# Gate and up as one product of 512 columns, three buffers of gathered rows, and the last two expert blocks placed on chip

## The chip, the cores and the metric

The kernel runs on one core of one Trainium2 chip. The metric is the device time of one execution in microseconds (us), measured over whole executions; a profile is taken of a further execution of the same program. The core has five engines that run their own instruction lists: TensorE (PE; the loading of its weights is listed as PEld), VectorE (DVE), ScalarE (ACT), GpSimd (POOL) and SyncE (SP, which here only issues transfers). Sixteen DMA engines move data between memory and the core's on-chip buffer.

## The reference, cut to what matters

One layer: a token mixer (retention and gated DeltaNet) and, behind it, a mixture of experts. 512 tokens of width 1024 go through the router; each token chooses 8 of 64 experts of inner width 256, and a shared expert is added. The change concerns the experts and what follows them:

```python
def expert_block(args):
    xe, e = args
    return (jax.nn.silu(xe @ w_gate_l[e]) * (xe @ w_up_l[e])) @ w_down_l[e]

yb = lax.map(expert_block, (xb, block_e)).reshape(n_slots, d)
routed = jax.ops.segment_sum(yb * slot_w[:, None], slot_tok, num_segments=t + 1)[:t]
shared = (jax.nn.silu(xt @ w_sh_gate_l) * (xt @ w_sh_up_l)) @ w_sh_down_l
return (routed + shared).reshape(b, l, d)
```

The sum is then normalised by its root mean square, scaled by a vector, and added to the residual stream x.

## The kernel before

The part in question starts at about 700 us. It walks over NE = 64 experts, one block of 128 gathered tokens each, and a 65th block that takes what one overfull expert has left (loop L1419, NE + 2 steps, since each step finishes the block of the step before). A dynamic loop (L1458) would serve further overfull blocks; on this data it runs zero times.

Per expert, SP loads gate, up and down weights of 1 MB each (L1193) into rings of three experts; the 65th comes by an indirect transfer of GpSimd (L1191). Products of float32 are made of three products of a rounded high part and a low part (mm3, L111 to L113). So each weight matrix is converted: ScalarE casts the high part (L1171, `wh`), VectorE subtracts it for the low part (L1173, `wl`), into a ring of seven buffers. GpSimd gathers the token rows with an indirect transfer (L1228, `xg`, six buffers; column 1024 + e of a row holds the token's weight for expert e). TensorE turns them (L1236), and ScalarE and VectorE write the high and low parts (L1238, L1239, `xT`). The projections (L1241) run 24 products of 256 columns for gate and then 24 for up. ScalarE and VectorE make the gated activation `sg` (L1248, L1249), TensorE turns it (L1256), ScalarE copies it (L1258, `aT`), and the down product follows (L1267, eight records of 512 columns in the trace). VectorE and ScalarE scale its halves by the token weight (L1271, L1269), and GpSimd adds the block to a sum in memory with an indirect, accumulating transfer (L1272), alternately to two sums, `accd[0]` and `accd[1]`; blocks 61 to 64 all go to `accd[1]`.

Within step e, in the order of the program: half of the projection of block e, a conversion, the turn of the activation of block e-1, the other half, the activation, a conversion, half of the turn of rows e+2, the down product of e-1 with its scatter, the other half of the turn, and the gather for e+4. A scheduler orders the instructions of an engine from this; each engine then runs its list strictly in order.

At the end `accd[0]` has been read at step 62 (L1453); after the branch around the dynamic loop, `accd[1]` is loaded (L1476), both are added (L1478), squared and summed (L1481), the inverse root is a power on GpSimd (L127), the result is scaled (L1484) and either added to the output by an accumulating transfer (L1486, two tiles of 128 tokens) or added on chip and stored (L1488, L1489, the other two).

## Time and profile before

| | |
|---|---|
| device time, median of 3 runs | 1408.96 us (1408.09 to 1412.23) |
| profiled execution, its own time | 1415.91 us |
| span in the profile | 1414.1 us |
| busy share of the span | PE 94%, PEld 76%, DVE 64%, ACT 46%, POOL 29% |
| moved by DMA | 340.5 MB, 241 GB/s over the span |
| mean granted TensorE clock | 0.971 of full speed |

The span is the time from the first to the last instruction of the profiled execution. Busy shares are means over stages of different kinds; what a change is worth is read in its own stage. "A <- B" in a list of waits says that A stood still until B was done. A chain is followed back from the last instruction, at each step to what released it; "DMA" in it is a transfer from its issue to its landing.

### The profile page before, as it was taken

Reading aid. Unit: us, or ns where it says so; the run is one execution under the profiler, and the core shown is the slowest. Engines: PE = TensorE matmul, PEld = TensorE weight load, DVE = VectorE, ACT = ScalarE, POOL = GpSimd, SP = SyncE. Lnnn points to the kernel's source line nnn. Section 1 sums busy time; section 2 is a strip of 40 time slices with the busy share of each in tenths; the row PEclk is TensorE's granted clock in tenths of the full one; section 3 lists DMA queues with packets and bytes.
Section 4 is the critical chain, followed back from the end, with each engine's and each line's share of the span. In section 5 each row is a group of like instructions: output and inputs, shape, how many; then the busy total and the mean of one; then the engine's idle time right before and its main releaser. Section 6 shows DMA issues by size and latency. Waiting matters only on the chain.

```text
span 1414.1 us, 20716 instructions
## 1 busy us (share of the span) xinstructions
PE 1324.8 (94%) x7848; PEld 1074.7 (76%) x7848; DVE 906.7 (64%) x1270; ACT 653.4 (46%) x926; POOL 409.6 (29%) x330
## 2 busy tenths in 40 slices
PE   6999988899999999999999999999999999999990
PEld 1678866798787777778888787878788888878770
DVE  5645796457676555547668666666666666666543
ACT  5533432553333222334355555555656565555531
POOL 0315544865321000003222222222222222224312
PEclk9899998999999999999999999999999999999995
DMA  7554411102316577575699999999999999999954
GB/s 275 181 141 117 121 56 35 52 16 74 88 49 179 178 214 223 152 259 195 249 386 349 352 370 345 373 351 364 362 366 361 368 364 361 367 364 338 326 183 127
DMA packets 137817, 340.51 MB, mean 241 GB/s; under 512 B 28218, under 2 KB 83038, under 8 KB 112756
## 3 DMA queue, kind: packets, MB, share of 16 engines
q1 hardware_dynamic: 110952, 289.46, 57.2%
q0 software_dynamic: 19584, 38.99, 10.9%
q10 hardware_dynamic: 7180, 10.72, 2.2%
q8 instruction: 63, 1.03, 0.3%
q14 instruction: 38, 0.31, 0.1%
HBM read 326.59 MB, written 48.31 MB: 265 GB/s over the span
## 4 chain that ended last, share of the span: by engine, by line
PE 43%; DMA 7%; issue 1%; ACT 1%; POOL 1%; DVE 0%; DVEq 0%; SPq 0%; ACTq 0%; POOLq 0%
PE cs L1267 13%; PE acc L111 7%; PE acc L113 7%; PE acc L112 7%; DMA w<-in_w_up_dram 4%; PE ci L1236 3%; DMA w<-in_w_gate_dram 2%; PE ci L1066 2%; PE acc L1078 1%; PE acc L1256 1%; DMA w<-acc 1%; POOL fr L127 0%; DMA acc<-y,slots 0%; DMA acc<-y,sl_i 0%; ACT wh L1171 0%
## 5 line engine op out<-in xcount | busy, mean ns | idle before, releaser
L111 PE MATMUL acc<-wh,xT 128*128 128x256 f32 x1040 | 302.2, 291 | 0.0
L113 PE MATMUL acc<-wh,xT 128*128 128x256 f32 x1040 | 291.0, 280 | 0.0
L112 PE MATMUL acc<-wl,xT 128*128 128x256 f32 x1040 | 290.6, 279 | 0.0
L1173 DVE TENSOR_TENSOR wl<-w,wh 128x2048 fp32r<-128x2048 f32 x88 | 201.5, 2291 | 76.2 <-PE acc L112 75.2
L1267 PE MATMUL cs<-wd,aT 128*128 128x512 f32 x520 | 234.6, 594 | 4.5 <-DMA wd<-in_w_down_dram 3.6
L1272 POOL DMA_INDIRECT acc<-y,slots x64 | 101.9, 1593 | 466.5 <-ACT y L1269 427.8
L1171 ACT CAST wh<-w 128x2048 fp32r<-128x2048 f32 x88 | 167.5, 1904 | 99.5 <-PE acc L113 70.2
L111 PEld LDWEIGHTS acc<-wh,xT 128*128 128x128 f32 x1040 | 196.6, 189 | 0.2 <-issue 0.2
L112 PEld LDWEIGHTS acc<-wl,xT 128*128 128x128 f32 x1040 | 196.1, 189 | 0.2 <-issue 0.2
L113 PEld LDWEIGHTS acc<-wh,xT 128*128 128x128 f32 x1040 | 195.5, 188 | 0.0
L1267 PEld LDWEIGHTS cs<-wd,aT 128*128 128x128 f32 x520 | 93.8, 190 | 99.0 <-issue 95.1
L1239 DVE TENSOR_TENSOR xT<-ci,xT 128x512 fp32r<-128x512 f32 x130 | 89.2, 687 | 96.5 <-ACT xT L1238 96.1
L100 ACT CAST wu<-raw 128x1024 fp32r<-128x1024 f32 (+1 forms) x73 | 75.1, 1036 | 104.6 <-DMA raw<-in_w_in_dram 68.0
L111 PE MATMUL acc<-hTx,wu 128*128 128x512 f32 (+1 forms) x296 | 119.6, 404 | 1.5 <-ACT wu L100 1.5
L113 PE MATMUL acc<-hTx,wu 128*128 128x512 f32 (+1 forms) x296 | 117.7, 398 | 1.5 <-DVE wu L107 1.5
L1173 DVE TENSOR_TENSOR wl<-wgu,wh 128x2048 fp32r<-128x2048 f32 x42 | 96.2, 2291 | 34.6 <-PE acc L112 34.4
L112 PE MATMUL acc<-hLx,wu 128*128 128x512 f32 (+1 forms) x296 | 117.1, 396 | 0.0
L107 DVE TENSOR_TENSOR wu<-raw,wu 128x1024 fp32r<-128x1024 f32 (+1 forms) x61 | 78.7, 1299 | 55.4 <-ACT wu L100 55.4
L1171 ACT CAST wh<-wgu 128x2048 fp32r<-128x2048 f32 x42 | 79.8, 1901 | 53.5 <-PE acc L113 35.5
L1236 PEld LDWEIGHTS ci<-ident,xg 128*128 128x128 f32 x520 | 72.5, 191 | 30.6 <-issue 30.2
L1228 POOL DMA_INDIRECT xg<-h2d,slots x64 | 75.5, 1180 | 35.6 <-issue 18.0
L1236 PE MATMUL ci<-ident,xg 128*128 128x128 f32 x520 | 78.7, 275 | 0.1
(493 smaller groups left out, 2374.3 us busy)
## 6 DMA issues: line engine op xcount, KB each, us to landing
wd<-in_w_down_dram SPq DMA_DIRECT2D x64, 1024.0 KB
w<-in_w_gate_dram SPq DMA_DIRECT2D x43, 1024.0 KB
w<-in_w_up_dram SPq DMA_DIRECT2D x43, 1024.0 KB
raw<-in_w_in_dram SPq DMA_DIRECT2D x56, 512.0 KB
wgu<-in_w_gate_dram SPq DMA_DIRECT2D x21, 1024.0 KB
wgu<-in_w_up_dram SPq DMA_DIRECT2D x21, 1024.0 KB
mraw<-in_w_mod_dram SPq DMA_DIRECT2D x32, 512.0 KB
wm<-in_w_mod_dram SPq DMA_DIRECT2D x16, 512.0 KB
```

Source lines behind the costliest of these rows:

```text
L100: nc.scalar.copy(dst, src)
L107: (self.nc.gpsimd if eng == "pool" else self.nc.vector).tensor_tensor(dst, src, hi.bitcast(F32), op=OP.subtract)
L111: mm(out, ah, bh, start=start, stop=False)
L112: mm(out, ah, bl, start=False, stop=False)
L113: mm(out, al, bh, start=False, stop=stop)
L1171: nc.scalar.copy(h[:, i:i + max(n, 1024)], w[:, i:i + max(n, 1024)])
L1173: eng(l[:, i:i + n], w[:, i:i + n], h[:, i:i + n].bitcast(F32), op=OP.subtract)
L1228: nc.gpsimd.indirect_dma_start(xg[:, :], None, self.h2d[:, :], bass.IndirectOffsetOnAxis(ap=ix, axis=0), bounds_check=511, oob_is_err=False)
L1236: nc.tensor.transpose(ps[:, k * 128:k * 128 + 128], xv[:, :, c * 4 + k], self.ident)
L1239: tt(l, ps, h.bitcast(F32), op=OP.subtract)
L1267: nc.tensor.matmul(ps, aT[:, m], wd[:, s], start=k == 0, stop=k == 1)
L1272: nc.gpsimd.indirect_dma_start(self.accd[acc][:, :], bass.IndirectOffsetOnAxis(ap=sx, axis=0), y[:, :], None, bounds_check=511, oob_is_err ...
```

## The change

Gate and up of an expert are converted into one pair of tiles (`GH`, `GL`, two experts deep), so that one product takes 256 columns of gate and 256 of up: 24 products of 512 columns in two halves of 12 (L111 to L113, called by `proj`). The cast is cut into two pieces of 1024 columns (L1188). The gathered rows have three buffers; the weight column is copied out of them (L1390, `wcol`). Blocks up to 62 are scattered as before, the last three of them to `accd[0]`. Blocks 63 and 64 are not scattered: their scaled results are kept as high and low parts (`down_parts`, L1293, L1294), one-hot matrices are made from their token lists (`places`, L1301), and TensorE adds them into place (`finish`, L1315, 32 products of 512 columns). `finish` then adds both sums (L1338), takes squares (L1342) and power (L1346), scales (L1349, one tile on GpSimd, L1345), adds x (L1352) and stores (L1353). All of x is loaded at step 62 (L1553), `accd[1]` at 63 (L1557), `accd[0]` at 64 (L1561). The dynamic loop now stands behind this and would repeat it.

```diff
...
 q = self.pool("mq", bufs=2, side="right", reuse=True)
 cst = lambda n: cons[n]
 xtile = lambda: q.tile([128, 2, 8, 128], F32R, name="xT", bufs=2)
-T8 = lambda name: self.wt8([128, 2048], F32R, name, "b")
-def conv(w, eng, n):
-    h, l = T8("wh"), T8("wl")
-    for i in range(0, 2048, max(n, 1024)):
-        nc.scalar.copy(h[:, i:i + max(n, 1024)], w[:, i:i + max(n, 1024)])
-    for i in range(0, 2048, n):
-        eng(l[:, i:i + n], w[:, i:i + n], h[:, i:i + n].bitcast(F32), op=OP.subtract)
-    return h, l
+self.w8s.close()
+self.w8as.close()
+wp = self.pool("wM", reuse=True)
+GU = [wp.tile([128, 2048], F32, name=f"wgu{i}") for i in range(4)]
+GH = [wp.tile([128, 2, 2048], F32R, name=f"gh{i}") for i in range(2)]
+GL = [wp.tile([128, 2, 2048], F32R, name="gl0"), self.hxpool.tile([128, 2, 2048], F32R, name="gl1", tag="b1")]
 hx = self.hxpool.tile([128, 2, 2048], F32, name="wgu", tag="b0")
-GU = [self.wt8([128, 2048], F32, "w", "a") for _ in range(4)] + [hx[:, 0], hx[:, 1]]
-wd2 = q.tile([128, 2, 2048], F32, name="wd", bufs=1)
-DW = [wd2[:, 0], wd2[:, 1], self.keep.tile([128, 2048], F32, name="wd", tag="k0")]
+GU += [hx[:, 0], hx[:, 1]]
+w2 = q.tile([128, 2, 2048], F32, name="wd", bufs=1)
+DW = [w2[:, 0], w2[:, 1], self.keep.tile([128, 2048], F32, name="wd", tag="k0")]
...
 raw = lambda e, n: DW[e % 3] if n == 2 else GU[(2 * e + n) % 6]
+def convert(e, n):
+    if e > NE:
+        return
+    w, h, l = raw(e, n), GH[e % 2][:, n], GL[e % 2][:, n]
+    for i in (0, 1024):
+        nc.scalar.copy(h[:, i:i + 1024], w[:, i:i + 1024])
+    tt(l, w, h.bitcast(F32), op=OP.subtract)
+    load(e + 3, n)
...
-for e, n in ((0, 0), (0, 1), (1, 0), (0, 2), (1, 1), (2, 0), (1, 2), (2, 1), (2, 2)):
+for e, n in ((0, 0), (0, 1), (1, 0), (1, 1), (0, 2), (1, 2), (2, 0), (2, 1), (2, 2)):
     load(e, n)
...
-xg6, xg3 = q.tile([128, 3, 1088], F32, name="xg", bufs=1), self.hxpool.tile([128, 3, 1088], F32, name="xg", tag="b1")
-xgs = [x[:, i] for x in (xg6, xg3) for i in range(3)]
+xg3 = q.tile([128, 3, 1088], F32, name="xg", bufs=1)
+xgs = [xg3[:, i] for i in range(3)]
...
 def gather(ix):
-    xg = xgs[ng[0] % 6]
+    xg = xgs[ng[0] % 3]
     ng[0] += 1
...
-def proj(out, x, w, first=True):
-    for k in range(8):
+def proj(out, x, e, ks=range(8)):
+    o = out.rearrange("p (n f) -> p n f", n=2)
+    for k in ks:
         s = slice(k * 256, k * 256 + 256)
-        self.mm3(out, x[0][:, k], x[1][:, k], w[0][:, s], w[1][:, s], k == 0, k == 7)
+        self.mm3(o, x[0][:, k], x[1][:, k], GH[e % 2][:, :, s], GL[e % 2][:, :, s], k == 0, k == 7)
...
+def down_half(aT, wd, c):
+    ps = self.pc()
+    for k in range(2):
+        s, m = slice(k * 1024 + c * 512, k * 1024 + c * 512 + 512), slice(k * 128, k * 128 + 128)
+        nc.tensor.matmul(ps, aT[:, m], wd[:, s], start=k == 0, stop=k == 1)
+    return ps
 def down(aT, sx, ws, wd, acc):
     y = self.rawp.tile([128, 1024], F32, name="y", tag="raw")
     for c in range(2):
-        ps = self.pc()
-        for k in range(2):
-            s, m = slice(k * 1024 + c * 512, k * 1024 + c * 512 + 512), slice(k * 128, k * 128 + 128)
-            nc.tensor.matmul(ps, aT[:, m], wd[:, s], start=k == 0, stop=k == 1)
+        ps = down_half(aT, wd, c)
         if c:
             nc.scalar.activation(y[:, 512:1024], ps, AF.Copy, scale=ws)
         else:
...
     nc.gpsimd.indirect_dma_start(self.accd[acc][:, :], bass.IndirectOffsetOnAxis(ap=sx, axis=0), y[:, :], None,
                                  bounds_check=511, oob_is_err=False, compute_op=OP.add)
-cv = {}
-def convert(e, n):
-    if e <= NE:
-        cv[e, n] = conv(raw(e, n), tt, 2048)
-        load(e + 3, n)
+def down_parts(aT, ws, wd, y):
+    for c in range(2):
+        ps = down_half(aT, wd, c)
+        h, l = y[:, c * 512:c * 512 + 512], y[:, 1024 + c * 512:1536 + c * 512]
+        nc.scalar.activation(h, ps, AF.Copy, scale=ws)
+        self.parted = nc.vector.scalar_tensor_tensor(l, ps, ws, h.bitcast(F32), op0=OP.mult, op1=OP.subtract)
+    return y
+def places(oh, row):
+    at = q.tile([128, 4], F32, name="at", bufs=2)
+    for t in range(4):
+        ts(at[:, t:t + 1], row, -128.0 * t, None, op0=OP.add)
+        ts(oh[:, t], cst("r0"), at[:, t:t + 1], None, op0=OP.is_equal)
+def finish(m, x1, blocks):
+    mg = [x[:, 0:1024] for x in xgs] + [self.rawp.tile([128, 1024], F32, name="mg", tag="raw")]
...
+    def place(t, j):
+        oh, y = blocks[j]
+        for c in range(2):
+            if j == 0:
+                PS[t, c] = self.pc() if t == 3 else self.pi() if c else self.pa()
+            for i in range(2):
+                nc.tensor.matmul(PS[t, c], oh[:, t], y[:, i * 1024 + c * 512:i * 1024 + c * 512 + 512],
+                                 start=j == 0 and i == 0, stop=j == len(blocks) - 1 and i == 1)
+    for t in (0, 1):
+        place(t, 0)
+    for t in range(4):
+        if t > 1:
+            place(t, 0)
+        for j in range(1, len(blocks)):
+            place(t, j)
...
+    def add(t):
+        for c in range(2):
+            s = slice(c * 512, c * 512 + 512)
+            then(lambda: tt(m[t][:, s], PS[t, c], m[t][:, s], op=OP.add))
+        self.d("moe", m[t], t)
+        junk = q.tile([128, 1024], BF, name="xT", bufs=2)
+        nc.scalar.activation(junk, m[t], AF.Square, scale=D ** -0.5, accum_out=r[:, t:t + 1])
+        nc.scalar.activation(r[:, t:t + 1], r[:, t:t + 1], AF.Identity, bias=self.eps)
+        if t == 1:
+            nc.gpsimd.tensor_tensor(mg[t], m[t], g2p, op=OP.mult)
+        nc.gpsimd.tensor_tensor(r[:, t:t + 1], r[:, t:t + 1], self.mhalf, op=OP.pow)
+    def scaled(t):
+        then(lambda: tt(mg[t], m[t], g2p, op=OP.mult))
+    def out(t, s, eng):
+        then(lambda: nc.vector.scalar_tensor_tensor(mg[t][:, s], mg[t][:, s], r[:, t:t + 1], x1[t][:, s], op0=OP.mult, op1=OP.add))
+        eng.dma_start(self.out[t * 128:t * 128 + 128, s], mg[t][:, s])
+    whole = slice(0, 1024)
+    add(0)
+    scaled(0)
+    add(1)
+    out(0, whole, nc.sync)
+    add(2)
+    scaled(2)
+    add(3)
+    out(1, whole, nc.scalar)
+    scaled(3)
+    out(2, whole, nc.sync)
+    out(3, slice(0, 512), nc.scalar)
+    out(3, slice(512, 1024), nc.sync)
...
     XG[e] = gather(SL[e])
     if e < NE:
-        W[e] = XG[e][:, 1024 + e:1025 + e]
+        W[e] = None
 def make(e, part):
     if e > NE:
         return
     if part == 0:
         XT[e] = xtile()
+        if W[e] is None:
+            W[e] = q.tile([128, 1], F32, name="wcol", bufs=4)
+            nc.scalar.copy(W[e], XG[e][:, 1024 + e:1025 + e])
     turn(XT[e], part, XG[e])
...
+    self.xrow = sl[0]
...
 x = lambda e: [XT[e][:, h] for h in range(2)]
+halves = lambda e: [raw(e, n)[:, i * 1024:i * 1024 + 1024] for n in range(2) for i in range(2)]
+Y = []
 for e in range(NE + 2):
+    if e == NE:
+        OH = GL[(NE - 1) % 2][:, 0, 0:1024].rearrange("p (b t n) -> p b t n", b=2, t=4)
...
+        places(OH[0], row)
+        places(OH[1], self.xrow)
...
     if e <= NE:
         pgu = self.pa()
-        proj(pgu[:, 0:256], x(e), cv[e, 0])
+        proj(pgu, x(e), e, range(4))
         convert(e + 1, 1)
     if e > 0:
         aT = turn_act(SG[e - 1])
     if e <= NE:
-        proj(pgu[:, 256:512], x(e), cv[e, 1])
+        proj(pgu, x(e), e, range(4, 8))
         SG[e] = act(pgu[:, 0:256], pgu[:, 256:512])
         convert(e + 2, 0)
     make(e + 2, 0)
-    if e > 0:
-        down(aT, SL[e - 1], W[e - 1], raw(e - 1, 2), 1 if e - 1 > NE - 4 else (e - 1) % 2)
+    if e > NE - 1:
+        Y.append(down_parts(aT, W[e - 1], raw(e - 1, 2), GH[(NE - 1) % 2][:, len(Y)]))
+    elif e > 0:
+        down(aT, SL[e - 1], W[e - 1], raw(e - 1, 2), (e - 1) % 2 if e < NE - 2 else 0)
         load(e + 2, 2)
     make(e + 2, 1)
     prepare(e + 4)
     if e == NE - 2:
-        halves = lambda w: [w[:, i * 1024:i * 1024 + 1024] for i in range(2)]
-        m0 = halves(raw(e, 0)) + halves(raw(e, 1))
-        x1 = halves(raw(e + 1, 0)) + halves(raw(e + 1, 1))
+        x1 = halves(NE - 2)
         for t in range(4):
-            nc.sync.dma_start(m0[t], self.accd[0][t * 128:t * 128 + 128])
+            nc.sync.dma_start(x1[t], self.out[t * 128:t * 128 + 128])
+    if e == NE - 1:
+        m1 = halves(NE)
+        for t in range(4):
+            nc.sync.dma_start(m1[t], self.accd[1][t * 128:t * 128 + 128])
+    if e == NE:
+        m = halves(NE - 1)
+        for t in range(4):
+            nc.sync.dma_start(m[t], self.accd[0][t * 128:t * 128 + 128])
+        with tc.issue_after(self.parted.ins):
+            for t in range(2):
+                tt(m[t], m[t], m1[t], op=OP.add)
         for t in range(2, 4):
-            nc.sync.dma_start(x1[t], self.out[t * 128:t * 128 + 128])
+            nc.gpsimd.tensor_tensor(m[t], m[t], m1[t], op=OP.add)
+finish(m, x1, list(zip(OH, Y)))
...
+    places(OH[0], self.xrow)
     xT, xg = xtile(), gather(ix)
     for c in range(2):
         turn(xT, c, xg)
     for n in range(3):
         load(NE, n, wi)
-    w = [conv(raw(NE, n), tt, 1024) for n in range(2)]
+        if n < 2:
+            convert(NE, n)
     pgu = self.pa()
-    for n in range(2):
-        proj(pgu[:, n * 256:n * 256 + 256], [xT[:, h] for h in range(2)], w[n])
-    down(turn_act(act(pgu[:, 0:256], pgu[:, 256:512])), ix, ws, raw(NE, 2), 1)
-m = halves(raw(NE, 0)) + halves(raw(NE, 1))
-r = q.tile([128, 4], F32, name="fr")
-for t in range(4):
-    (nc.scalar if t % 2 else nc.sync).dma_start(m[t], self.accd[1][t * 128:t * 128 + 128])
-for t in range(4):
-    tt(m[t], m[t], m0[t], op=OP.add)
-    self.d("moe", m[t], t)
-    junk = q.tile([128, 1024], BF, name="xT", bufs=2)
-    nc.scalar.activation(junk, m[t], AF.Square, accum_out=r[:, t:t + 1])
-    self.rsqrt(r[:, t:t + 1], r[:, t:t + 1], 1.0 / D, EPS)
-for t in range(4):
-    nc.vector.scalar_tensor_tensor(m[t], m[t], r[:, t:t + 1], g2p, op0=OP.mult, op1=OP.mult)
-    if t < 2:
-        nc.gpsimd.dma_start(self.out[t * 128:t * 128 + 128], m[t], accum_op=OP.add)
-    else:
-        tt(m[t], m[t], x1[t], op=OP.add)
-        (nc.scalar if t % 2 else nc.sync).dma_start(self.out[t * 128:t * 128 + 128], m[t])
+    proj(pgu, [xT[:, h] for h in range(2)], NE)
+    aT = turn_act(act(pgu[:, 0:256], pgu[:, 256:512]))
+    y = down_parts(aT, ws, raw(NE, 2), GH[(NE - 1) % 2][:, 0])
+    finish(m, x1, [(OH[0], y)])
...
```

ScalarE, one step in the middle of the loop; `wh` and `gh` are the high parts of weights. Before:

```order
L1171 CAST wh<-wgu 128x2048
L1258 COPY aT<-acc 128x256
L1248 ACTIVATE sg<-acc 128x256
L1171 CAST wh<-wgu 128x2048
L1238 CAST xT<-ci 128x512
L1269 ACTIVATE y<-cs,xg 128x512
L1238 CAST xT<-ci 128x512
```

After:

```order
L1390 COPY wcol<-xg 128x1
L1188 CAST gh_5609<-wgu_5606 128x1024
L1267 COPY aT<-acc 128x256
L1188 CAST gh_5609<-wgu_5607 128x1024
L1257 ACTIVATE sg<-acc 128x256
L1188 CAST gh_5609<-wgu_5606 128x1024
L1245 CAST xT<-ci 128x512
L1188 CAST gh_5609<-wgu_5607 128x1024
L1282 ACTIVATE y<-cs,wcol 128x512
L1245 CAST xT<-ci 128x512
```

The casts are four instead of two, the weight column stands ahead of the first, and that ahead of `aT`. Three casts now stand behind `aT`.

VectorE at the end, from the last down product on. Before:

```order
L1271 TENSOR_SCALAR y<-cs,sl_w 128x512
L1459 REGISTER_ALU
L1459 COMPARE_AND_BRANCH
L1459 UNCONDITIONAL_BRANCH
L1478 TENSOR_TENSOR w<-w,wgu 128x1024 x3
L126 TENSOR_SCALAR fr<-fr 128x1
L1478 TENSOR_TENSOR w<-w,wgu 128x1024
L126 TENSOR_SCALAR fr<-fr 128x1 x2
L1484 SCALAR_TENSOR_TENSOR w<-w,fr,g2p 128x1024
L126 TENSOR_SCALAR fr<-fr 128x1
L1484 SCALAR_TENSOR_TENSOR w<-w,fr,g2p 128x1024 x3
L1488 TENSOR_TENSOR w<-w 128x1024 x2
```

After, where `m` lies in the `wgu` tiles and `mg` partly in `xg`:

```order
L1294 SCALAR_TENSOR_TENSOR gh_5609<-cs,wcol,gh_5609 128x512 x2
L1564 TENSOR_TENSOR wgu_5604<-wgu_5604,wgu_5606 128x1024 x2
L1294 SCALAR_TENSOR_TENSOR gh_5609<-cs,sl_w,gh_5609 128x512 x2
L1338 TENSOR_TENSOR wgu_5604<-acc,wgu_5604 128x512
L1338 TENSOR_TENSOR wgu_5604<-ci,wgu_5604 128x512
L1349 TENSOR_TENSOR xg<-wgu_5604,g2p 128x1024
L1338 TENSOR_TENSOR wgu_5604<-acc,wgu_5604 128x512
L1338 TENSOR_TENSOR wgu_5604<-ci,wgu_5604 128x512
L1352 SCALAR_TENSOR_TENSOR xg<-xg,fr,wgu 128x1024
L1338 TENSOR_TENSOR wgu_5605<-acc,wgu_5605 128x512
L1338 TENSOR_TENSOR wgu_5605<-ci,wgu_5605 128x512
L1349 TENSOR_TENSOR xg<-wgu_5605,g2p 128x1024
```

The branch (L1459) stood ahead of the sums; now sums, scaling and final pass alternate by tile, and the branch follows behind the rows shown.

GpSimd at the end, from the scatter of the dynamic loop on. Before:

```order
L1272 DMA acc_4919<-y,sl_i 512x1024
L1459 REGISTER_ALU
L1459 COMPARE_AND_BRANCH
L1459 UNCONDITIONAL_BRANCH
L127 TENSOR_TENSOR fr<-fr,mhalf 128x1 x3
L1486 DMA out_dram<-w 128x1024
L127 TENSOR_TENSOR fr<-fr,mhalf 128x1
L1486 DMA out_dram<-w 128x1024
```

After, from the scatter of block 59 on, where `acc_4918` is `accd[0]`:

```order
L1285 DMA acc_4919<-y,slots 512x1024
L1285 DMA acc_4918<-y,slots 512x1024
L1198 DMA wd<-in_w_down_dram,wi 128x2048
L1285 DMA acc_4918<-y,slots 512x1024 x2
L1566 TENSOR_TENSOR wgu_5605<-wgu_5605,wgu_5607 128x1024 x2
L1346 TENSOR_TENSOR fr<-fr,mhalf 128x1
L1345 TENSOR_TENSOR xg<-wgu_5604,g2p 128x1024
L1346 TENSOR_TENSOR fr<-fr,mhalf 128x1 x3
L1571 TENSOR_LOAD nx
```

Ahead of the rows of before stand, outside the loop, the scatters of blocks 61, 62, 63 and 64. The scatters of 63 and 64 and both accumulating stores are gone; two sums and a scaling over 1024 columns stand ahead of the powers.

## Rows read from the trace of the kernel before

**Rows 1.** Busy us by stretch: PE, PEld, DVE, ACT, POOL; clock, DMA share, GB/s

```profile
800.00:900.00 100.00, 100.00 (x655) 81.81 (x654) 66.66 (x61) 57.99 (x70) 26.32 (x20) 1.00 1.01 363
...
1200.00:1300.00 100.00, 99.43 (x652) 81.54 (x652) 65.34 (x57) 57.30 (x68) 29.04 (x20) 1.00 1.00 362
...
1380.00:1414.10 34.10, 1.46 (x4) 0.38 (x2) 12.82 (x15) 5.27 (x9) 8.07 (x7) 0.55 0.47 130
```

**Rows 2.** The chain that ended last, from 1225 us (start, us, what)

```profile
1237.03 3.44 PE cs L1267 x8
...
1247.23 3.44 PE cs L1267 x8
...
1259.27 25.89 DMA w<-in_w_gate_dram
...
1319.03 29.25 DMA w<-in_w_up_dram
...
1377.71 4.65 DMA acc<-y,slots
...
1389.12 8.80 DMA w<-acc
```

**Rows 3.** The waits from 800 to 1250 us (in total, times, longest)

```profile
DVE wl L1173 <- PE acc L112: 91.7, 89, 1.2
```

**Rows 4.** The waits from 1250 to 1360 us

```profile
ACT wh L1171 <- DMA w<-in_w_up_dram: 19.1, 4, 5.7
```

**Rows 5.** Timeline of TensorE in an expert step (start, us, form)

```profile
989.83 0.28 PE L111 MATMUL acc<-wh,xT 128*128 128x256 f32 x1
...
991.47 0.28 PE L113 MATMUL acc<-wh,xT 128*128 128x256 f32 x1
```

**Rows 6.** Timeline of TensorE in an earlier stage with 512 columns

```profile
469.82 0.39 PE L112 MATMUL acc<-hLx,wu 128*128 128x512 f32 x1
...
473.96 0.39 PE L112 MATMUL ci<-yl,wu 128*128 128x512 f32 x1
```

**Rows 7.** Timeline of ScalarE ahead of the down product of 1247.23

```profile
1245.57 0.36 ACT L1258 COPY aT<-acc 128x256 f32<-128x256 f32 x1
```

**Rows 8.** Timeline of GpSimd, a gather behind that product

```profile
1253.58 1.04 POOL L1228 DMA_INDIRECT xg<-h2d,slots  x1 [0.31 <-issue]
```

**Rows 9.** Tile of gathered rows: ns min/median/max, first and last start

```profile
L1236 PE MATMUL ci<-ident,xg x520: 272/274/347, 707.1 to 1357.8; 128*128 128x128 f32 x174
L1228 POOL DMA_INDIRECT xg<-h2d,slots x64: 993/1039/2473, 697.8 to 1317.7; - x64
```

**Rows 10.** Groups by line and form: count, busy us, mean ns, idle before

```profile
L100 ACT CAST wu<-raw 128x1024 fp32r<-128x1024 f32 x72 | 74.9, 1047 | 104.6 <-DMA raw<-in_w_in_dram 68.0 <-DMA raw<-in_w_ret_out_dram 13.3 <-PE acc L113 8.7
...
L1116 POOL TENSOR_TENSOR h<-mix,mrow 128x512 f32<-128x512 f32 x4 | 7.1, 1787 | 5.8 <-DVE mix L1112 2.9 <-PE ci L1019 1.5 <-issue 1.5
...
L1101 DVE TENSOR_TENSOR mix<-acc,mrow 128x512 f32<-128x512 f32 x8 | 5.4, 687 | 15.6 <-ACT ojunk L1100 15.6
...
L1484 DVE SCALAR_TENSOR_TENSOR w<-w,fr,g2p 128x1024 f32<-128x1024 f32 x4 | 5.0, 1281 | 0.7 <-POOL fr L127 0.7
L127 POOL TENSOR_TENSOR fr<-fr,mhalf 128x1 f32<-128x1 f32 x4 | 5.0, 1262 | 14.6 <-DVE fr L126 14.6
...
L1478 DVE TENSOR_TENSOR w<-w,wgu 128x1024 f32<-128x1024 f32 x4 | 4.8, 1221 | 15.0 <-DMA w<-acc 15.0
...
L548 POOL TENSOR_TENSOR QE<-QE,rk 128x512 f32<-128x512 f32 x4 | 4.1, 1039 | 0.0
```

**Rows 11.** Timeline of the end, all engines

```profile
1377.76 3.70 PE L1267 MATMUL cs<-wd,aT 128*128 128x512 f32 x8 [0.82 <-ACT aT L1258]
...
1393.08 2.36 DVE L1478 TENSOR_TENSOR w<-w,wgu 128x1024 f32<-128x1024 f32 x2 [12.55 <-DMA w<-acc]
...
1408.58 0.34 ACTq L1489 DMA_DIRECT2D out_dram<-w  x1
```

**Rows 12.** Timeline of GpSimd near the end, a scatter that waits

```profile
1369.86 1.56 POOL L1272 DMA_INDIRECT acc<-y,slots  x1 [9.02 <-DMA acc<-y,slots]
```

16 lines of the change are left out of this document (15 added, 1 removed).

## The prediction

> **What bounds the kernel now.** I read the profile in this order: busy time by stretch, the chain that ended last, the waits, then timelines of one step and of the end. From 800 to 900 us, and nearly so up to 1300, TensorE is busy without a gap while the DMA engines are busy too, at 363 GB/s [rows 1]. In this stage the kernel walks over the experts, one step every 1247.23 − 1237.03 = 10.20 us [rows 2]. The ten waits listed from 800 to 1250 us name no load; the largest behind TensorE is VectorE waiting for a weight buffer that TensorE still reads [rows 3]. So here TensorE sets the step. After 1257 us the chain leaves TensorE: a gate load takes 25.89 us and an up load 29.25 us to land [rows 2], and from 1250 to 1360 ScalarE stands four times for an up load, 19.1 us in all [rows 4]. The last 100 us of the loop go by the loads. The last expert product ends at E = 1377.76 + 3.70 = 1381.46 [rows 11]; the span ends at 1414.1, so 32.6 us run with TensorE practically idle at a granted clock of 0.55 [rows 1]: a chain of scatter, loads, sums, powers, scaling and stores.
>
> **The change part by part.** (a) Products. Start to start, 256 columns take (991.47 − 989.83)/14 = 0.117 us [rows 5] and 512 columns of the same number type (473.96 − 469.82)/18 = 0.230 us [rows 6]. A step now has 48 × 0.117 = 5.62 us of them and will have 24 × 0.230 = 5.52. Two for one is therefore nearly nothing: 0.10 us a step, 65 steps, 6.6 us at most. The rest of a step (turns, down product) is unchanged.
>
> How much of this lands? Up to 1250 us, 53 of the 65 steps, the loads have room, so TensorE should be about 5 us ahead there. Then the loads set the pace, and they come ahead only as far as the DMA engines, already at a share of 1.01 [rows 1], can take it. Against this, both halves of an expert's weights are now converted in the same step, so up must have landed nearly a step earlier than now. I take −2 us for the loop, between 0 and −6.6; a loss of 2 is possible if the late loads bite earlier.
>
> (b) The gathered rows. Three buffers instead of six do not hold back the gather: the rows of expert e+1 have been read when those of e+4 are fetched. But ScalarE now copies the weight column out of the rows before it casts the first half of the gate weights, and behind that stands aT, for which the down product waits. Queued behind a late gather are thus that cast, aT, and through aT TensorE. A gather goes out 1253.58 − 1247.23 = 6.35 us after a down product starts [rows 2, 8]; aT starts 1.66 us before it (1245.57) [rows 2, 7]. The cast before it is half of what it was, so 1.05 us by the cast of 1024 columns [rows 10], and the copy some 0.2. Two steps of 10.10 us after its own down product the rows must be there by 20.2 − 1.66 − 1.25 = 17.3 us; aT itself lasts 0.36, so with no slack left for it another 1.2 us later: 18.5 us. The gather has 18.5 − 6.35 = 12.1 us. No row gives its landing in the loop. Below it is bounded by the first one, issued at 697.8, its rows turned at 707.1: 9.3 us [rows 9]. Above, the turn now needs the rows just before the down product, 20.4 − 0.45 − 6.35 = 13.6 us, and never waited for them [rows 3]. Between 9.3 and 13.6 I take the lower half, since the first one ran beside loads too, and cost it at nothing. The gain covers that; each us beyond 12.1 would cost 0.5 us a step.
>
> (c) The end. What goes: two scatters in sequence (4.65 us of the chain for the first alone) and 8.80 us of loads behind them [rows 2]. What comes: the parts of the last two blocks, 32 products of 512 columns, and a chain on VectorE. Worked from E: the placing of block 63 stands ahead of the last down product, which moves that by some 1.3 us. The parts of block 64 take two passes over 512 columns, 0.69 each [rows 10], and four products 0.9: the first sum could start at E + 3.7. Do the sums in memory arrive by then? The scatter of block 62 went out at 1369.86 after waiting for its forerunner [rows 12], E − 11.6; landing like the next one, 4.65, it is done by E − 7. The first two loads of the sums were there at 1393.08, 4.0 us after the load's row of 1389.12, the last 8.80 after it [rows 2, 11]: E − 3 and E + 1.8. They are in time.
>
> VectorE then runs 8 sums at 0.69, 3 scalings at 1.22, 3 final passes at 1.28 and two of half that size: 14.4 us if nothing holds it [rows 10]. GpSimd may: it adds sums for two tiles and multiplies one, three passes over 1024 columns. It has none of these in the trace, only 512 columns at 1.04 to 1.79 us, so 2.1 to 3.6 each [rows 10]. Added up in queue order with powers of 1.26 us [rows 10], the first power ends at E + 7.7 to 9.0, the second at E + 11.0 to 13.8; VectorE, which needs the first at E + 7.7, ends at E + 18.1 to 19.5. From the last store's issue to the end of the span were 5.5 us [rows 11]; this gives E + 23.6 to 25.0, against 32.6. The branch around the extra loop now lies behind the stores; it may show for up to 1.5 us. I take −7 for the end, between −3 and −9.
>
> The GPSIMD Engine Reference of the Trainium skill (section 3.1) measures a float32 sum over 2048 columns at 4.5 us, from which 2.25 us for 1024 is an estimate. With it the end would be at the lower bound, E + 23.6, and the time 1 to 2 us shorter. No row shows it; the sum keeps both bounds.
>
> **Sum.** The profiled execution took 1415.91 us with a span of 1414.1; the median of the runs is 1408.96, 7 us below. Loop −2 and end −7 give 1415.9 − 9 = 1406.9 for that execution, and on the median 1408.96 − 9 = 1400.
>
> **The rivals.** *The loop gains nothing.* The DMA engines stand at a share of 1.01 and 363 GB/s all along [rows 1]. If they cannot go faster, a shorter step only makes loads late sooner; only the end gains: 1409 − 7 = 1402. Against it: no wait for a load before 1250 [rows 3]. The Trainium skill's DMA: Bandwidth & Descriptors (section Where 436 GB/s comes from) has memory bind at about 358 GB/s per core, which is this case; the row, at 363, lies just above it.
>
> *The whole gain lands.* The late loads are no harder than now, the loop gives 6.6 and the end 9: 1393.5. For it: TensorE without a gap over hundreds of us. Against: the last stage is paced by loads that land in 25 to 29 us.
>
> *The end gives little.* GpSimd's passes at 3.6 us, sums in memory that land 3 to 5 us late because the loads of x and of both sums now crowd the last steps, and the branch: end −2.5, loop −1, so 1405.5.
>
> *Slower: the late gather.* If gathers land after 12.1 us, ScalarE holds aT and TensorE stops once a step. The loop equals the present one at 12.3 us, and the end's gain is eaten at 12.6. At 13.0 us, 0.45 × 62 steps = 28, less the 7 of the end: 1430.
>
> The fifth, that a product of 512 columns costs two of 256, is already nearly so in (a), and moves the time by 6.6 us at most.
>
> **How the numbers follow.** Forecast (1400) 0.38; loop gains nothing (1402) 0.20; whole gain 0.17; the end gives little 0.16; late gather 0.09. A measurement of this kernel tells about 0.3% (4.2 us) from no change: faster is below 1404.7, slower above 1413.2. Faster: 0.36 + 0.17 + 0.17 + 0.03 = 0.73. Same: 0.02 + 0.03 + 0.13 + 0.02 = 0.20. Slower: 0.07. The range runs from 1388 (whole gain, with part of the late stalls gone) to 1412 (little at the end and a few late gathers).
>
> **What would show it.** Starts of down products 10.1 us apart in the middle; waits of ScalarE for loads from about 1240 on, as long as now; no wait of the weight-column copy for a gather above 0.2 us (a row of it by the ten would be the slower rival); TensorE's last product before the placing at about 1380, and 24 to 26 us from there to the end, VectorE waiting for GpSimd's power once or twice. I am wrong if steps are longer than 10.2 us, or if between that product and the end more than 30 us pass.

## The result, and the profile after

| | before | after |
|---|---|---|
| device time, median (4 runs each) | 1409.72 us (1408.09 to 1412.23) | 1419.55 us (1418.82 to 1421.42) |
| ratio after / before | | 1.0077, 95% interval 1.0052 to 1.0102 |
| profiled execution, its span | 1415.91, 1414.1 us | 1421.42, 1419.6 us |
| start of the first down product | 726.0 us | 726.7 us |
| first down product's start to the last one's end ("the loop") | 655.5 us | 661.8 us |
| from there to the end of the span ("the end") | 32.7 us | 31.2 us |

The change made the kernel 0.8% slower, where 0.6% faster was forecast (1400, between 1388 and 1412). In the profiled executions the 5.5 us more are 0.7 ahead of the experts, 6.3 in the loop, and 1.5 less at the end.

The busy time by stretch, as in [rows 1] (PE, PEld, DVE, ACT, POOL; clock, DMA share, GB/s), of after:

```profile
800.00:900.00 100.00, 100.00 (x419) 71.23 (x418) 66.84 (x61) 62.17 (x100) 45.70 (x20) 1.00 1.01 361
1100.00:1200.00 100.00, 97.26 (x402) 68.21 (x401) 61.23 (x55) 57.33 (x93) 40.98 (x20) 1.00 0.98 353
1200.00:1300.00 100.00, 93.92 (x386) 66.11 (x385) 62.72 (x56) 57.93 (x94) 38.97 (x19) 1.00 0.97 345
1300.00:1380.00 80.00, 75.39 (x302) 52.70 (x301) 48.03 (x51) 39.67 (x65) 27.42 (x14) 0.98 0.86 290
1388.50:1419.60 31.10, 8.30 (x28) 5.99 (x26) 19.88 (x20) 6.47 (x13) 12.66 (x7) 0.69 0.32 122
```

From 800 to 900 us TensorE is busy throughout, as before. Between 1200 and 1300 us it now lacks 6.1 us where [rows 1] lacked 0.6. The waits from 800 to 1250 us (in total, times, longest), as in [rows 3], name the reason:

```profile
DVE sg L1258 <- ACT sg L1257: 131.1, 43, 4.9
...
ACT gh L1188 <- DMA wgu<-in_w_up_dram: 50.0, 17, 4.8
```

In before's list no load stood up to 1250 us; now ScalarE stands 17 times for the up weights. The timeline of TensorE shows both regimes in the starts of the down products (start, us, form, idle before and what ended it):

```profile
959.40 3.60 PE L1274 MATMUL cs<-wd,aT 128*128 128x512 f32 x8
969.51 3.60 PE L1274 MATMUL cs<-wd,aT 128*128 128x512 f32 x8
```
```profile
1227.77 3.67 PE L1274 MATMUL cs<-wd,aT 128*128 128x512 f32 x8 [0.33 <-DMA wd<-in_w_down_dram]
1238.97 3.70 PE L1274 MATMUL cs<-wd,aT 128*128 128x512 f32 x8 [0.84 <-ACT aT L1267]
```

At 960 us the step is 10.11 us (10.085 in the mean of two neighbouring steps; [rows 2] gave 10.20). At 1230 us it is 11.20. ScalarE's timeline has the cause inside that long step:

```profile
1226.99 0.35 ACT L1267 COPY aT<-acc 128x256 f32<-128x256 f32 x1
1231.58 1.05 ACT L1188 CAST gh<-wgu 128x1024 fp32r<-128x1024 f32 x1 [4.24 <-DMA wgu<-in_w_up_dram]
1232.54 0.38 ACT L1257 ACTIVATE sg<-acc 128x256 f32<-128x256 f32 x1
```

The cast of the next up weights waits 4.24 us for its load, and the activation stands behind it in ScalarE's list. The first long step starts at 1151 us; the kernel is 4.2 us ahead of before there (down product 42 at 1151.1 against 1155.3), and at down product 63 it is 7.0 us behind (1380.1 against 1373.1).

The end, as in [rows 11], from the last down product on, with the scatter of block 62 ahead of it:

```profile
1379.53 1.55 POOL L1285 DMA_INDIRECT acc<-y,slots  x1 [7.04 <-DMA acc<-y,slots]
...
1384.84 3.62 PE L1274 MATMUL cs<-wd,aT 128*128 128x512 f32 x8
1385.95 2.13 SPq L1561 DMA_DIRECT2D wgu<-acc  x4
...
1389.51 1.22 DVE L1564 TENSOR_TENSOR wgu<-wgu,wgu 128x1024 f32<-128x1024 f32 x1 [4.28 <-DMA wgu<-acc]
1391.76 1.23 DVE L1564 TENSOR_TENSOR wgu<-wgu,wgu 128x1024 f32<-128x1024 f32 x1 [1.02 <-DMA wgu<-acc]
1392.90 1.41 DVE L1294 SCALAR_TENSOR_TENSOR gh<-cs,sl_w,gh 128x512 fp32r<-128x512 f32 x2
...
1393.75 4.74 POOL L1566 TENSOR_TENSOR wgu<-wgu,wgu 128x1024 f32<-128x1024 f32 x2 [12.67 <-issue]
...
1394.53 0.69 DVE L1338 TENSOR_TENSOR wgu<-acc,wgu 128x512 f32<-128x512 f32 x1 [0.23 <-PE acc L1315]
...
1396.53 3.03 DVE L1349 TENSOR_TENSOR xg<-wgu,g2p 128x1024 f32<-128x1024 f32 x1
...
1400.85 3.32 POOL L1345 TENSOR_TENSOR xg<-wgu,g2p 128x1024 f32<-128x1024 f32 x1 [0.85 <-DVE wgu L1338]
...
1411.32 0.33 SPq L1353 DMA_DIRECT2D out_dram<-mg  x1
```

The last down product ends at E = 1388.46. VectorE waits until E + 1.0 for the accumulator (1389.51), holds the parts of block 64 back behind two sums (1392.90), and starts the first sum of `finish` at E + 6.1. The last store goes out at E + 22.9; the span ends 8.3 us later.

### The profile page after: what moved, and what is told of

Read it like the earlier page. It is cut to its first block, busy times and chain, and to the rows that moved or that the text cites. A ratio compares the mean times of both kernels' runs of the same rounds, so it can differ in the third digit from the quotient of the medians.

```text
span 1419.6 us, 17702 instructions
## 1 busy us (share of the span) xinstructions
PE 1326.0 (93%) x6320; PEld 1005.0 (71%) x6320; DVE 908.8 (64%) x1293; ACT 672.8 (47%) x1126; POOL 513.7 (36%) x326
## 5 line engine op out<-in xcount | busy, mean ns | idle before, releaser
L1188 ACT CAST gh<-wgu 128x1024 fp32r<-128x1024 f32 x260 | 271.7, 1048 | 158.2 <-DMA wgu<-in_w_up_dram 87.3
L1189 DVE TENSOR_TENSOR gl<-wgu,gh 128x2048 fp32r<-128x2048 f32 x130 | 297.2, 2287 | 36.6 <-ACT gh L1188 31.1
L1235 POOL DMA_INDIRECT xg<-h2d,slots x64 | 147.2, 2300 | 314.4 <-DVE y L1284 176.7
L111 PE MATMUL acc<-gh,xT 128*128 128x512 f32 x520 | 215.3, 414 | 0.0
L113 PE MATMUL acc<-gh,xT 128*128 128x512 f32 x520 | 204.8, 394 | 0.0
L112 PE MATMUL acc<-gl,xT 128*128 128x512 f32 x520 | 203.8, 392 | 0.0
L1285 POOL DMA_INDIRECT acc<-y,slots x63 | 133.4, 2118 | 95.4 <-ACT wcol L1390 40.0
L1258 DVE TENSOR_TENSOR sg<-sg,acc 128x256 f32<-128x256 f32 x65 | 27.4, 421 | 193.5 <-ACT sg L1257 193.3
L111 PE MATMUL acc<-hTx,wu 128*128 128x512 f32 (+1 forms) x296 | 118.7, 401 | 2.8 <-ACT wu L100 1.5
L113 PE MATMUL acc<-hTx,wu 128*128 128x512 f32 (+1 forms) x296 | 117.0, 395 | 2.0 <-DVE wu L107 2.0
L113 PEld LDWEIGHTS acc<-gh,xT 128*128 128x128 f32 x520 | 97.6, 188 | 22.2
L111 PEld LDWEIGHTS acc<-gh,xT 128*128 128x128 f32 x520 | 98.8, 190 | 16.7 <-issue 0.2
L112 PEld LDWEIGHTS acc<-gl,xT 128*128 128x128 f32 x520 | 98.2, 189 | 16.8 <-issue 0.2
L1245 ACT CAST xT<-ci 128x512 fp32r<-128x512 f32 x130 | 75.8, 586 | 0.0
```

What stands on the lines that cost most here:

```text
L111: mm(out, ah, bh, start=start, stop=False)
L112: mm(out, ah, bl, start=False, stop=False)
L113: mm(out, al, bh, start=False, stop=stop)
L1188: nc.scalar.copy(h[:, i:i + 1024], w[:, i:i + 1024])
L1189: tt(l, w, h.bitcast(F32), op=OP.subtract)
L1235: nc.gpsimd.indirect_dma_start(xg[:, :], None, self.h2d[:, :], bass.IndirectOffsetOnAxis(ap=ix, axis=0), bounds_check=511, oob_is_err=False)
```

## The experiments

Times and lengths in us. A time is a median of 4 to 10 runs, or of one where the table says "1 run"; "before there" is before on the same chip and in the same session (its median, or one run beside e8 to e11 and e15). The lengths come from one profile each: "step" is the mean from down product 5 to 35, of which in e9 alone some are held up; "loop" and "end" are as above.

| kernel | time | before there | step | loop | end |
|---|---|---|---|---|---|
| before | 1409.72 | | 10.21 | 655.5 | 32.7 |
| after | 1419.55 | 1409.72 | 10.10 | 661.8 | 31.2 |
| half_a, half_b (1 run) | 1395.80, 1402.56 | 1407.54 | 10.10, 10.21 | 643.2, 650.5 | 29.4, 32.6 |
| e1_late | 1414.22 | 1407.54 | 10.10 | 662.7 | 29.0 |
| e2_nofor | 1412.22 | 1407.54 | 10.10 | 660.8 | 27.4 |
| e5_aslow (1 run) | 1423.82 | 1410.24 | 10.23 | 666.6 | 31.0 |
| e6_bfast (1 run) | 1406.41 | 1410.24 | 10.09 | 652.4 | 31.1 |
| e7_front | 1405.97 | 1410.24 | 10.28 | 658.1 | 26.9 |
| e8_bgather3 (1 run) | 1417.06 | 1412.04 | 10.24 | 652.2 | 32.4 |
| e9_scatfirst (1 run) | 1448.73 | 1412.04 | 10.77 | 698.0 | 28.8 |
| e10_apart (1 run) | 1419.49 | 1409.03 | 10.30 | 666.6 | 26.8 |
| e11_places (1 run) | 1415.63 | 1409.03 | 10.10 | 662.1 | 30.0 |
| e12_turned | 1400.02 | 1407.14 | 10.10 | 643.2 | 31.1 |
| e13_bturned (1 run) | 1408.07 | 1407.14 | 10.21 | 650.5 | 31.2 |
| e14_best | 1397.18 | 1407.14 | 10.10 | 643.2 | 27.4 |
| e15_by16 (1 run) | 1395.53 | 1407.56 | 10.10 | 643.2 | 27.0 |

The experts begin between 718 and 731 us in profiles of kernels that are the same up to there; so the loop and the end are compared, and not the times of single runs.

**Is it the loads?** Both kernels with half of each down load from expert 3 on; the other half of the down weights stays what it was.

```diff
-nc.sync.dma_start(t, a[NAMES3[n]][0, e].rearrange("(p k) f -> p (k f)", p=128))
+c = 1024 if n == 2 and e > 2 else 2048
+nc.sync.dma_start(t[:, 0:c], a[NAMES3[n]][0, e].rearrange("(p k) f -> p (k f)", p=128)[:, 0:c])
```

> The changed kernel with only the first half of each down weight loaded (experts 3 to 63; the second half of the buffer is stale, so the down products are of wrong data): one sixth of the loads is gone. If late loads are what stretches the steps after 1150 us (theories W and D alike): all steps 10.06 to 10.11 us to the end, last down product ending at about 1370, 18 us below the changed kernel. If something else stretches them (a late gather, TensorE itself): steps of 10.5 to 12 us stay.

> The kernel before with only the first half of each down weight loaded (as in half_a, wrong data in the down products). Late loads as the limit of its last 100 us: all steps 10.2 us, last down product ending at about 1376 instead of 1381.5. Together with half_a it gives the loop's gain where loads have room: 63 steps of 0.12, so 7 to 7.5 us in favour of the changed kernel; if the 512-column product gains nothing by itself, 0.

All steps are then equal, and the loops take 643.2 and 650.5 us. So late loads cost before 5.0 us of its loop and after 18.6; and the joint product with room to run is worth 7.3 us.

**The conversions' place in the queue** (e1_late): the casts of both halves stand behind the activation and the second turn, so that a late load holds neither.

```diff
-                convert(e + 2, 0)
+                with tc.issue_after(self.silu.ins):
+                    convert(e + 2, 0)
...
+            with tc.issue_after(self.turned.ins):
+                convert(e + 2, 1)
```

> The changed kernel with only the order of conversions altered: both casts of gate are queued behind the activation of the step, both casts of up behind the second turn of the step, two steps ahead of their use as before; nothing is left out. Theory W (window): the loop lost 11 us after 1150 us because the casts, cut in halves and tied to the halves of the projection, hold a weight buffer some 10.7 us for up (first cast to end of subtraction) instead of about 4.3, so that a load must land within 22 to 23 us, and a late one stands in ScalarE's queue ahead of the activation. Then the last down product ends at 1380 to 1383 us instead of 1388.5, steps are still 10.09 us until about 1220, and the time is 5 to 8 us below that of the changed kernel (1412 to 1415). Theory D (rate): the DMA engines cannot serve a step of 10.09 us, whatever the order; then the last down product stays within 2 us of 1388.5 and the time within 2 us of 1419.5.

The loop stays at 662.7: the loads themselves are late, whatever stands behind them. The time fell further than theory D allowed, to 1414.22 (before there took 2.2 us less, too), but not in the loop; the end is 2.2 us shorter in its profile.

**The pace** (e5_aslow adds to after a 256-column product a step, overwritten at once; e6_bfast leaves one 256-column product per expert out of before):

```diff
+            if ks[0] == 0:
+                nc.tensor.matmul(o[:, 0], x[0][:, 0], GH[e % 2][:, 0, 0:256], start=True, stop=True)
```

> The changed kernel with one product of 256 columns more in each step (its result is overwritten at once, so nothing is left out): the undisturbed step goes from 10.09 to about 10.2 us, as before. From the first to the end of the last down product the kernel before took 655.5 us, the changed one 661.8. Theory P (pace): what hurts is that a shorter step asks for the loads faster than the slowest DMA engine serves them, and the late loads then cost more than the pace gave; at 10.2 us this stretch falls back to 655 to 657 us. Theory Q (pattern): the changed kernel's order of transfers (three loads within 3.5 us, gather and scatter apart) burdens the slowest engine whatever the pace; the stretch stays at 661 us or more.

> The kernel before with one product of 256 columns left out per expert (the high-by-low product of one eighth of gate, so its result is slightly off): the undisturbed step goes from 10.20 to 10.09 us. Theory P: the stretch from the first to the end of the last down product grows from 655.5 to 659 us or more, long steps beginning well before 1257 us. Theory Q: it stays at 655 us or less, the loads being as early as before.

After at before's step still has its long steps, from about 1140 us on (666.6); before at after's step gains 3 us. Asking for weights faster is not enough to lose time. It does eat up part of what it gains: 63 steps of 0.13 us less should have given before 8 us. Without long steps e6_bfast's loop would be about 650.5 − 8 = 642.4 us and e5_aslow's about 643.2 + 8 = 651.5 (estimates from half_b, half_a and the steps), so long steps cost them some 10 and 15 us.

**Parts of the change** (e8_bgather3 gives before three gather buffers and the copied weight column; e10_apart takes the joint product of after apart again; e11_places swaps two allocations of after):

```diff
-self.mm3(o, x[0][:, k], x[1][:, k], GH[e % 2][:, :, s], GL[e % 2][:, :, s], k == 0, k == 7)
+self.mm3(out, x[0][:, k], x[1][:, k], GH[e % 2][:, n, s], GL[e % 2][:, n, s], k == 0, k == 7)
```

> The kernel before with the gather side of the change alone: three buffers, the weight column copied out by ScalarE; nothing left out. The stretch from the first to the end of the last down product was 655.5 us before and 661.8 changed. Theory G (gather side: three buffers, the copy, GpSimd's queue): it grows to 659 us or more here, with steps over 10.3 us beginning before 1250 us. Theory H (weights' side: pair tiles, split casts, order and closeness of the loads): it stays within 1.5 us of 655.5.

> The changed kernel with the 512-column products taken apart again: the gate product whole, then the up product whole, 256 columns each, in the order of the kernel before, but out of the paired tiles, with three buffers of gathered rows, the weight column's copy and the new end. Full function. Theory S (the joint product itself makes the loads slower: both halves of a pair are read over the whole step): undisturbed steps of 10.21 us, hardly any long steps, first down product to last 652 to 656 us. Theory B (what came with it, the paired tiles' places, the gather's buffers and the column's copy): steps of 10.21 us and long steps from about 1140 us on as in the changed kernel, 661 to 667 us.

> The changed kernel with the order of two allocations changed: the converted pairs stand ahead of the four loaded weight tiles in the pool, so that loads and casts write to other addresses of the scratchpad. Nothing else differs. If the addresses make the loads slower: first down product to last is off from 661.8 by more than 4 us, and where the loads get quicker, 650 to 656 us. If they don't: 660 to 664 us and long steps from about 1140 us on.

652.2, 666.6 and 662.1 us: neither the gather's buffers nor the joint product nor those addresses make the loads later. Before with the gather's side alone came out 3.3 us shorter, below what either of its theories had expected; why was not looked into. Taken apart, the products cost the loop another 4.8 us.

**The late gather** (e9_scatfirst: after with each scatter ahead of the next gather on GpSimd):

```diff
-            prepare(e + 4)
+                with tc.issue_after(self.scat.ins):
+                    prepare(e + 4)
```

> The changed kernel with GpSimd's queue in the order of the kernel before: the scatter of a step ahead of its gather (nothing left out). Theory G: the stretch shrinks from 661.8 to 658 us or less. Theory H: it stays within 1.5 us of 661.8. A third way: the later gather holds the weight column and with it the activation, steps above 10.15 us from the start, and the stretch grows beyond 664.

The wait list from 800 to 1250 us has what the rival of that name described:

```profile
ACT wcol L1390 <- DMA xg<-h2d,slots: 132.0, 35, 7.4
```

The step grows to 10.77 us and the loop by 36 us. In after this wait does not occur; there the gathers land in time (issue to landing, 800 to 1250 us, from the view of the tile `xg`):

```profile
DMA to landing us min/median/max: 7.8/10.3/12.6
```

**Which part of a load is late?** A load of 1 MB reports its landing in 16 parts. The Trainium skill's DMA: Bandwidth & Descriptors (section Why a DMA increments its semaphore by 16 and not by 1) says that these are the 16 DMA engines, which finish independently; the events of this trace agree in that the 16 parts come at times of their own. The parts of expert 43's down load, us after its issue, sorted:

```
before    6.6  6.6  6.6  6.6  6.8  7.1  7.8  8.6  8.9  9.2  9.6  9.7 11.3 12.7 16.1 18.1
after     7.3  7.5  7.6  7.6  7.7  7.8  7.8  7.8  7.9  8.1  9.5 10.3 10.5 16.6 24.8 25.1
e12       7.3  7.3  7.4  7.4  7.5  7.8  7.9  8.2  8.5  9.1  9.2  9.5  9.5 10.1 12.2 12.3
e15       7.2  7.3  7.3  7.3  7.4  7.6  8.4  8.5  8.7  8.8  9.2  9.4  9.8 10.1 10.5 12.5
```

In after, 13 engines are through after 10.5 us; three lag, two of them by 17 us. The mean DMA share, 0.98 from 1100 to 1200 us, hides this. Something is dealt unevenly. It is hardly the loads, which the trace shows in 128 equal pieces of 8192 bytes, eight an engine if they are dealt evenly. It can be the gathered and scattered rows: a list has 128 slots, of which 64 hold a token on average, and each half is filled from its first slot on. So the lists were turned round, expert by expert, with nothing else changed (e12_turned on after, e13_bturned on before):

```diff
-nc.vector.tensor_copy(both[0:64, 0:64], first[0:64])
-nc.vector.tensor_copy(both[64:128, 64:128], first[64:128])
+for r in range(4):
+    for h in range(2):
+        rows, c, o = slice(64 * h, 64 * h + 64), 128 * r + 64 * h, (4 * r + 8 * h) % 16
+        nc.vector.tensor_copy(both[rows, c + o:c + 64], first[rows, 0:64 - o])
...
+    nc.tensor.matmul(ps[:, r:64:4], both[:, 128 * r:128 * r + 128], cst("i2")[:, r:64:4], start=True, stop=True)
```

> The changed kernel with the slots of each expert's list turned round: every half of a list begins 0, 4, 8 or 12 slots further on, by the expert's number modulo 4, the second half 8 further than the first. Full function; the same rows, bytes, transfers and instructions in the loop. In the changed kernel 13 of a load's 16 parts land within 11 us of its issue around expert 43 and the last three after 16 to 25 us, so two or three of the 16 DMA engines fall behind; a list fills each half from slot 0, and if slot k is moved by engine k modulo 16, the first engines carry some 5 row pairs an expert and the last 3. Theory U (uneven rows): with the lists turned no engine falls behind by more than some 7 us at expert 43, its down load lands within 17 us, first down product to last takes 644 to 651 us (661.8 in the changed kernel), and the whole 1403 to 1409 us. Theory T (the transfers as a whole got slower with the change, rows don't matter): landing 22 to 27 us, 660 to 664 us, 1417 to 1421 us.

> The kernel before with the same turning of the lists. Full function. Theory U: its late long steps go, first down product to last 650.5 to 652.5 us (655.5 before; 650.5 is what it took with half of each down load), the whole 1404 to 1408 us beside 1409. Theory T: 654.5 to 656.5 us, no change.

Both loops fall to exactly what half the down load gave, 643.2 and 650.5 us: no long step is left. (The one run of e13_bturned took 1408.07 us beside 1407.14 of before there; its 5.0 us show in the loop alone.) The windows of e12_turned:

```profile
1100.00:1200.00 100.00, 100.00 (x419) 71.23 (x418) 66.86 (x61) 62.20 (x100) 45.72 (x20) 1.00 1.01 369
1200.00:1300.00 100.00, 100.00 (x419) 71.23 (x418) 67.37 (x60) 62.20 (x100) 44.42 (x20) 1.00 1.00 369
```

TensorE has no gap left, and the engines together move 369 GB/s where after moved 353 and 345. The ratio of e12_turned to before is 0.9943 (0.9916 to 0.9969).

**How the rows are dealt.** e15_by16 turns every second list by 16 slots only (`o = 16 * r`, r = 0 or 1):

> The changed kernel with every second expert's list turned by 16 slots in both halves, the others as they are. Full function. It tells two maps of slots to DMA engines apart. Map M (engine = slot modulo 16, as e12_turned was reckoned): a turn by 16 changes no engine's rows, so nothing changes: down load of expert 43 landing after 22 to 27 us, 660 to 664 us from first to last down product. Map S (blocks of four slots: the first half of a list goes to engines 0 to 7, the second to 8 to 15, engine by the slot's number over 4, modulo 8): a turn by 16 moves the surplus four engines on, the heaviest engines carry 4.8 rows an expert instead of 5.7: landing within 15 us at expert 43, and 643 to 648 us.

643.2 us: not map M, by which nothing would have changed, but what map S had foretold. Map S is the one that the Trainium skill's DMA: Bandwidth & Descriptors (section The descriptor swizzle) gives for a plain transfer to 128 partitions; here the gathered and scattered rows follow it too. By this map and the reference's own routing of this data, the heaviest engine carries 5.7 rows an expert and the lightest 2.1. With 24 pieces of loads at the trace's mean of 0.335 us and 0.43 us a row (fitted; gather and scatter packets add up to 0.50 in the means) the four slowest engines would be 15.9, 14.6, 8.5 and 6.1 us behind at expert 43 of after; the list above has 17.6, 17.3, 9.1 and 3.0 beyond 7.5. The heights are partly the fit's doing; the pattern of two engines far behind the others is not. Reckoned the same way, slot modulo 16 leaves its worst engine 6.5 us behind, and eight neighbouring slots to an engine leave four engines 55 to 60 us behind.

**The end.** e2_nofor is after without the loop for further blocks, which on this data never runs. e7_front is before's loop with the new end, where that loop stands ahead of the sums and adds on chip, and the scatters alternate to the last. e14_best joins e12_turned with that end.

```diff
-        cnt = nc.values_load(nx[0:1, 0:1], min_val=0, max_val=62)
-        with tc.For_i(0, cnt) as _:
...
-            finish(m, x1, [(OH[0], y)])
```

> The changed kernel without the dynamic loop over further overfull blocks (it runs zero times on this data, so nothing of the work done is missing). Theory F: behind the stores, the branch waits until they have landed and only then does GpSimd begin its closing drain (3.55 us in the trace of the changed kernel, from 1415.25), so the end is 3.5 to 4.5 us earlier: about 1415.5. Rival: the landing of the last store sets the end and the branch hides behind it; then under 1 us.

> The loop of the kernel before (256-column products, six gather buffers) with the changed end (blocks 63 and 64 placed on chip), the scatters alternating to the last so that block 62 need not wait for 61, and the dynamic loop put ahead of the sums, where it adds into them on chip; nothing is left out. If the end's change is good and the loop's is what cost the time: the stretch of the down products stays near 655 us, from the last down product to the end 26 to 28 us instead of 32.7, the time 5 to 6 us below the kernel before. If placing on chip itself gives nothing: within 2 us of the kernel before.

> The changed kernel's loop with turned lists and the end of e7_front: scatters go to the two accumulators in turn to the last, the loop for further blocks stands ahead of the sums and adds on chip, and the residual rows are loaded after it. Full function. Theory U: 644 to 651 us of loop and an end of about 27 us (26.9 in e7_front), 1397 to 1404 us, faster than all full kernels so far. Theory T: 660 to 664 us of loop, 1411 to 1417 us.

e7_front against before: 0.9974 (0.9956 to 0.9991). e14_best: 0.9925 (0.9896 to 0.9955); its 1397.18 us beat both kernels. From the last store's issue to the end pass 8.3 us in each of nine kernels with the branch behind the stores (after, half_a, e1, e5, e9, e10, e11, e12, e15), and 3.6 in e2, e7 and e14. The events of after show why: the engines leave the branch at 1415.2 us, when the last store has landed (1414.9), and only then does GpSimd begin its closing drain of 3.55 us. In e2_nofor the drain begins at 1403.9, ahead of the last store (1407.2). What comes ahead of the store depends on when the accumulator lands. In e15_by16 it is there early (the view begins behind the first of its four loads):

```profile
1361.92 1.37 SPq L1565 DMA_DIRECT2D wgu<-acc  x3
...
1365.22 2.44 DVE L1568 TENSOR_TENSOR wgu<-wgu,wgu 128x1024 f32<-128x1024 f32 x2 [1.73 <-DMA wgu<-acc]
...
1385.44 0.33 SPq L1357 DMA_DIRECT2D out_dram<-mg  x1
```

Its last down product ends at 1366.72 (1363.09 and 3.62). VectorE's sums start before that, and the last store goes out at E + 18.7. In e14_best the loads of the residual come later, the sums start only 2.7 and 3.6 us behind E, and VectorE and GpSimd sum at the same time; E = 1365.96:

```profile
1368.68 5.69 POOL L1594 TENSOR_TENSOR wgu<-wgu,wgu 128x1024 f32<-128x1024 f32 x2 [14.12 <-DMA wgu<-acc]
...
1369.56 5.89 DVE L1592 TENSOR_TENSOR wgu<-wgu,wgu 128x1024 f32<-128x1024 f32 x2 [2.10 <-issue]
...
1389.67 0.33 SPq L1357 DMA_DIRECT2D out_dram<-mg  x1
```

The store goes out at E + 23.7: 5.0 us are lost ahead of the store, and 4.7 gained behind it. With e15_by16's sums and e14_best's branch the end would be 18.7 + 3.6 = 22.3 us, an estimate that no run tested.

## Why the prediction was wrong

**(a) The product: right.** 0.10 us a step from [rows 5, 6]; the steps shrank from 10.21 to 10.10. With room the loop gains 7.3 us, a little above the 6.6 that the text allowed at most.

**(a) "How much of this lands?": the step that failed.** It said that the loads have room up to 1250 us, that TensorE would then be 5 us ahead, and that the loop nets −2. TensorE was 4.2 us ahead, but the loads bit 100 us earlier, from 1151 us, and the loop lost 6.3. The text reckoned room in time, from a list of waits that named no load [rows 3]. A backlog makes no wait until it is used up: in before the down load's last part already landed 10.1 us after issue at expert 15, 13.8 at 35 and 23.2 at 51. The loads of 25.89 and 29.25 us in the chain [rows 2] were its end, and I took them for a trait of the last stage. The DMA share of 1.01 [rows 1] was read as all engines being full, while a few were overfull. "A loss of 2 is possible if the late loads bite earlier" named the sign and the way, not the size.

**The rival "the loop gains nothing"** had the mechanism: a shorter step only makes loads late sooner. It set the loss at nothing, as if the loads' speed were fixed by the memory at 363 GB/s. It wasn't: after itself moved 369 from 1000 to 1100 us, before its long steps, and with the lists turned the 369 holds up to 1300. The figure beside it, about 358 GB/s from the Trainium skill's DMA: Bandwidth & Descriptors (section Where 436 GB/s comes from), is passed in every window shown whose steps are all undisturbed (361 to 369).

**What stays open.** Long steps cost after 18.6 us and before 5.0. A shorter step uses up the room of the loads sooner, and e5_aslow and e6_bfast tell how much that is: before at after's step loses some 10 us, after at before's step some 15. So the shorter step accounts for 4 to 5 of the 13.6 us between the two, and for no loss by itself, as e6_bfast's loop still gained 3. The other 9 to 10 us, which made the gain a loss, are left to the new weight side, by exclusion: e8_bgather3 has the whole gather side of after, the gather ahead of the scatter included, and its loads are not later. The slowest engine's landings of gate loads, expert 8 to 43, are 10.40 us apart in before, 10.29 to 10.45 in e6 to e8, but 10.48 to 10.60 in after, e1, e2, e5, e10 and e11. So in these single profiles it is slower, by some 0.1 us an expert, in every kernel with the paired tiles, at any pace, with the joint product or without (e5, e6 and e7 ran on one chip); the nearest two of the groups are 0.03 apart. Which part of the new weight side does it was not found. With even lists no load is late enough to make a long step.

**(b) The gather: right.** It cost nothing: its instruction goes out 4.8 us behind a down product (6.35 was reckoned), its rows land 12.6 us later at most, and the weight column never waited for them from 800 to 1250 us. That these rows load some of the DMA engines more than others, and so make the weights late, was not thought of, and that decided.

**(c) The end: −7 forecast, −1.5 measured.** Counted from the end of the last down product, the sum had 2.4 + 14.4 + 5.5 = 22.3 us at the least and the trace has 6.1 + 16.8 + 8.3 = 31.2. (That is one profile; kernels with the same end have 26.8 to 31.2. The 1.3 us by which the placing was to move the last down product came to 0.1: 1384.84 − 1380.12 = 4.72, and in before 1377.76 − 1373.12 = 4.64.) Three terms failed. First, the accumulator "in time": the scatter of block 62 was put at E − 11.6 and went out at E − 8.9 (1379.53, after 7.04 us for its forerunner); its loads followed at 1385.95, 6.4 us later and not 4.65. VectorE therefore started its first sum at E + 6.1, and not at the 2.4 (3.7 from the old E) of the text, with the parts of block 64 queued behind sums in memory. Where the accumulator was early (e15_by16) the last store went out at E + 18.7; the text's 18.1 to 19.5 from the old E is 16.8 to 18.2 from the new. Second, the branch: up to 1.5 us forecast, for which no row stood; with it 8.3 us pass behind the last store's issue and without it 3.6, so it costs 4.7. In the sum it shows as 8.3 instead of 5.5. Third, 1.22 us for a scaling on VectorE became 3.03 beside GpSimd's sums (1396.53), part of the 16.8 us that its chain took instead of 14.4. GpSimd's own passes, bounded at 2.1 to 3.6, came at 2.37 (a sum) and 3.32 (the scaling). The Trainium skill's GPSIMD Engine Reference (section 3.1) led to an estimate of 2.25 us: the 2.37 agrees within 0.12; the 3.32, beside VectorE's sums and final passes, does not.
